# A gate's projection between the two halves of each pair's q and k, and every block of logits tied to a share of the pair's projections

## The chip, the core and the metric

The kernel runs on one core of a Trainium2 chip. The metric is the device time of one execution in microseconds (us). Five engines with queues of their own appear below: PE (matrix multiplies, with its weight loads shown apart as PEld), DVE (VectorE), ACT (ScalarE), POOL (GpSimd) and SP (which issues most DMAs). Each engine works through its own list in order.

## The reference, cut to what matters

One block with two mixers, for 1024 tokens of width 1024, in float32:

```python
h = _rmsnorm(x, norm_g)
u = h @ w_in                                   # all projections at once
u_a, u_b, u_g = split(u)                       # RWKV, forgetting attention, gates
y_a = _rwkv7_mixer(u_a, ...) @ w_out_a         # 8 heads of 64: a recurrence over the tokens
y_b = _fox_mixer(u_b, ...) @ w_out_b           # 8 heads of 64: causal softmax attention
merged = sigmoid(g_a) * y_a + sigmoid(g_b) * y_b
return _rmsnorm(x + merged @ w_out, final_norm_g)

# _fox_mixer: q and k are normalised per head, then for each block of queries
logits = q @ k.T * scale + cum[q] - cum[k]     # cum: running sum of log forget gates
p = softmax(where(causal, logits, -inf)); o = p @ v
```

## The kernel before, in words

All matrix products run as three products of split operands (high times high, high times low, low times high), so a projection of 128 columns for 512 tokens is 24 matmuls into one PSUM bank (`project`, L326 to L333). The transposed, normalised input lies on chip as `hTH` and `hTL`. The kernel has two kinds of work on PE. **Bulk**: projections that need nothing but `hT` and weights, namely r, k, v of the RWKV heads, 24 gate tiles (`gate_tile`, tiles `ps_gg`), v of the attention (`project_v`, `pfv`), and q and k of each pair of attention heads (`project_qk`, `pf`). **Latency-bound** work: small steps that wait for DVE, ACT or DMA after each matmul.

The RWKV part runs in four units (two groups of heads times two halves of the tokens). `prep` builds a unit's operands; its core is a triangular inverse made by a long series of DVE steps (`etmp`, `lt`, L663 and L667), a round trip through DRAM, then 32 small matmuls `pw` (L687), a copy by ACT, 32 more `pz` (L698), and a copy by ACT into `Tb`. `chain` then walks eight chunks; each step is `px` (L724), DVE, `pu` (L739), DVE, `po` (L749), DVE, and the next step needs the state that this one leaves. `norm_out` normalises a unit's output and ends in transposes `pt` (L796).

The attention goes by four pairs of heads. `project_qk` computes q and k of a pair for all tokens in eight blocks of 128 tokens; `norm_qk` scales them per head and transposes them, half of the tokens at a time (`pqk`, `pqq`, L971): the scaling of the first half is on POOL, of the second half on DVE (L967). The transposed q must also reach the other partitions, by a DMA on chip (`QA`, L988 and L989), and its low part goes through DRAM (`qlo`, L986, then `QZ`, L1002). `attend` takes blocks of 256 queries: logits `sc` (L1024 with `QA`, L1025 with `QZ`, L1029 the mask), a minimum on DVE (L1031), the exponential on ACT (L1035), a scaling on DVE (L1039), transposes `pt` (L1048) and the product with v, `po` (L1068, L1069). `merge` and the output projection follow.

A scheduler sets each engine's order when the program is built, by priorities: latency-bound work goes in as soon as it is ready in the scheduler's reckoning, bulk fills what is left. Where its reckoning would place a step too early, `not_before` ties the step to a place in the list of bulk matmuls (`laid_`); such a tie fixes the order on PE and makes nothing wait by itself. Gate tiles left over after the RWKV units (`RFILL`) are spread over the four pairs by `FPRE` and `FFILL`.

The weights have three slots of high and low parts (`WB`) and one landing buffer (`RB`). The projections of the RWKV and early attention part rotate over three PSUM banks (`RTAGS`).

Of the kernel before, what the change touches and what calls it, by code (L numbers as in the profile page):

```python
# [18 lines left out]
P = 128  # L19
S = 1024  # L20
# [31 lines left out]
QKFIRST = True  # L52
LATER = 1000000
PLACE = {
    "pw0_0": 179, "pw0_1": 294, "pw1_0": 398, "pw1_1": 502,
}
PACE = 0.3
PHPOOL = True
# [12 lines left out]
PACE0 = 0.0  # L71
WA1 = 0
MGB = 3
NQEARLY = True
ATTFIRST = True
T1B = 3
RFILL = [5, 5, 3, 3]
FPRE = [1, 0, 0, 2]
FFILL = [1, 2, 2, 0]


def rsqrt_newton(nc, y, x, t):
# [12 lines left out]
def kernel(  # L95
# [212 lines left out]
    transposed(1, range(KD))  # L308
    xctx.close()

    laid_ = []

    def laid(ins):
        laid_.append(ins.ins)

    def not_before(first, name):

        if name not in PLACE:
            return
        for ins in first:  # L320
            tc.add_manual_dep(
                ins, laid_[PLACE[name]].name,
                mybir.DependencyInfo(mybir.DependencyClass.NoSync, mybir.DependencyReason.DATA),
                reason="not_before",
            )
# [173 lines left out]
    def prep(pp_, n):  # L499
# [191 lines left out]
        for e, _, q1, q2 in half:  # L691
            nc.scalar.copy(TW[q2].rearrange("p c s -> p (c s)"), pw[q2, :])
        pz = ps_misc(f"pz{u}")
        for h in range(2):
            for c in range(UC):
                g = UC * h + c
                for e, _, q1, q2 in half:
                    nc.tensor.matmul(pz[q1, g * HB : (g + 1) * HB], TW[q2, g, :], Tb[q2, c, h, q2], start=True, stop=True)  # L698
        for e, _, q1, q2 in half:
            nc.scalar.copy(Tg[q1, :, :, q2], pz[q1, :].rearrange("p (h c t) -> p h c t", h=2, t=HB))  # L700
        return dict(AR=AR, Q=Q, BKt=BKt, SV=SV, AK=AK, WC=WC, bV=bV, s2c=s2c, lnw=lnw, pw=mms, sc=late_sc, pt=[])

    states = [rp.tile([P, 2, 2, C], F32, tag=f"state{j}", name=f"state{j}") for j in range(2)]
    for t in states:
# [129 lines left out]
    def project_v(cb):  # L834


        VC = 264
        KH = KD // 2
        ncol = VC if cb == 0 else 256
        c0 = COL_FV + 256 * cb  # L840
        vs_ = []
        for p in (2 * cb, 2 * cb + 1):
            vparts[p] = fpa[0].tile([P, 8, 2, P], F32R, tag="V", name=f"V{p}", bufs=VB)
            vs_.append(vparts[p])
        parts = []
        for kh in range(2):
            rs_ = slice(kh * KH * P, (kh + 1) * KH * P)
            wH = wpool.tile([P, KH, VC], F32R, tag="wH", name=f"wvH{cb}_{kh}", bufs=WB)[:, :, :ncol]
            wL = wpool.tile([P, KH, VC], F32R, tag="wL", name=f"wvL{cb}_{kh}", bufs=WB)[:, :, :ncol]
            w = wpool.tile([P, KH, VC], F32, tag="w", name=f"wv{cb}_{kh}", bufs=RB)[:, :, :ncol]  # L850
            nc.sync.dma_start(
                w[:, :, 0:256], w_in2[rs_, c0 : c0 + 256].rearrange("(k p) c -> p k c", p=P)
            )
            if cb == 0:
                nc.sync.dma_start(
                    w[:, :, 256:VC], w_in2[rs_, COL_FF : COL_FF + 8].rearrange("(k p) c -> p k c", p=P)
                )
# [52 lines left out]
    def project_qk(p):  # L910
# [41 lines left out]
        return xn, rr  # L952

    def norm_qk(p, xn, rr):
# [6 lines left out]
        cb = [rp.tile([P, S], F32, tag=("AK", "bV")[h], name=f"cb{p}_{h}") for h in range(2)]  # L961
        for h in range(2):
            src = cumd[8 * (2 * p + h) : 8 * (2 * p + h) + 8].rearrange("(o b) t -> o (b t)", o=1)
            nc.sync.dma_start(cb[h], src.broadcast_to([P, S]))
# [25 lines left out]
        return KA, QA, qlo, cb  # L990

    sc_tags = SCTAGS

    def attend(p, KA, QA, qlo, cb):
        for i in range(4):
            nb = 2 * i + 2

# [8 lines left out]
            for h, q in ((0, A), (1, B)):  # L1006
# [3 lines left out]
                for e in range(2):  # L1010
# [6 lines left out]
                    for g in range(ng):  # L1017
# [6 lines left out]
                        nc.tensor.matmul(sc[:, :mw], QA[:, h, qs], KA[:, h, ms], start=True, stop=False)  # L1024
# [131 lines left out]
    for i, (p, n) in enumerate(units):  # L1156
# [3 lines left out]
        with bulky():  # L1160
# [4 lines left out]
            if i + 1 == len(units):  # L1165
                project_v(0)
                forget()
                qk = project_qk(0)
        not_before(d["pw"], f"pw{p}_{n}")
        not_before(d["sc"], f"sc{p}_{n}")  # L1170
        if i:
            not_before(before["pt"], "pt%d_%d" % units[i - 1])
        before = d
        with order(-LATER):
            yv = chain(p, n, d)
        with order(LATER // 2 if i + 1 < len(units) else -LATER):
            norm_out(p, n, d, yv)
    bulk_tags[:] = FTAGS
    qk = norm_qk(0, *qk)
    def bulk_fox(p, nxt):  # L1180
        with bulky():
            fill(FPRE[p], 0)
            if p < 3:
                nxt = project_qk(p + 1)
            if p < 3 and NQEARLY:
                nxt = norm_qk(p + 1, *nxt)
            fill(FFILL[p], 0)
            if p < 3 and not NQEARLY:
                nxt = norm_qk(p + 1, *nxt)
        if p == 1 and ATTFIRST:  # L1190
            with order(LATER):
                project_v(1)
        return nxt

    for p in range(4):
        if not ATTFIRST:
            nxt = bulk_fox(p, None)
        with order(-LATER):
            attend(p, *qk)
        if ATTFIRST:  # L1200
            nxt = bulk_fox(p, None)
        qk = nxt
        if p == 0 and not ATTFIRST:
            with order(LATER):
                project_v(1)
# [68 lines left out]
```

## Time and profile before

| | |
|---|---|
| median of 3 runs | 1139.93 us (1131.49 to 1140.08) |
| profiled execution | 1135.76 us |
| its span, first to last instruction | 1133.9 us |
| PE busy | 1052.9 us, 93% of the span |
| DVE, ACT, POOL busy | 709.2, 459.9, 317.0 us |
| mean granted clock of PE | 0.968 of full speed |

The rows further down come from that one execution; times in them count from the start of its span. PE has two clock levels, 2.4 GHz (1.00) and 1.2 GHz (0.50); PEclk is the mean of what was granted in a stretch.

### The profile page before, as it was taken

To read this page: it belongs to the slowest core of one execution; us is meant where nothing else is said; L and a number is where in the kernel's file an instruction comes from. 1 tells how busy PE (TensorE), PEld (TensorE's weight loads), DVE (VectorE), ACT (ScalarE), POOL (GpSimd) and SP (SyncE) were. 2 spreads that over 40 slices of the span, in tenths; PEclk is the share of its full clock that TensorE was granted. 3 is DMA by queue.
4 is the path that set the end of the run, shared out by engine and by line. 5 is a ranking of instruction groups with operands and counts; after the bars stand their busy time and mean duration, and the time that the engine had idled before them with its cause. 6 is when DMAs were issued, how large, how long until landed. Compare 5 with 4: busy or idle time off the path is not lost. (4 is left out here: it accounts for less than half of the span.)

```text
span 1133.9 us, 18405 instructions
## 1 busy us (share of the span) xinstructions
PE 1052.9 (93%) x6591; PEld 871.7 (77%) x6591; DVE 709.2 (63%) x1855; ACT 459.9 (41%) x969; POOL 317.0 (28%) x467
## 2 busy tenths in 40 slices
PE   4989999999899999997998989979997999999997
PEld 3867777777677777777887877968896887887885
DVE  7414776699648883796678858652736823475145
ACT  6534323534243314431546636443544623223122
POOL 4420522252213421231113223222132222244400
PEclk9999999999989899998999989989998999999999
DMA  6256444144422433222024213232223126645133
GB/s 214 59 172 216 123 103 121 40 119 134 113 74 76 127 103 99 62 82 66 20 77 125 85 49 83 85 88 80 92 59 89 55 77 188 217 134 178 64 102 121
DMA packets 126684, 118.21 MB, mean 104 GB/s; under 512 B 33489, under 2 KB 91970, under 8 KB 126594
## 3 DMA queue, kind: packets, MB, share of 16 engines
q1 hardware_dynamic: 114304, 94.99, 29.1%
q10 hardware_dynamic: 11714, 21.52, 5.1%
q8 instruction: 52, 0.85, 0.3%
q0 software_dynamic: 576, 0.54, 0.2%
q14 instruction: 38, 0.31, 0.1%
HBM read 79.23 MB, written 35.68 MB: 101 GB/s over the span
## 5 line engine op out<-in xcount | busy, mean ns | idle before, releaser
L331 PE MATMUL ps_gg<-hTH,wH_gg 128*128 128x512 f32 x384 | 160.0, 417 | 0.8 <-DVE ql L982 0.6
L332 PE MATMUL ps_gg<-hTL,wH_gg 128*128 128x512 f32 x384 | 160.2, 417 | 0.0
L333 PE MATMUL ps_gg<-hTH,wL_gg 128*128 128x512 f32 x384 | 159.1, 414 | 0.0
L210 POOL TENSOR_TENSOR wL_gg<-w_gg,wH_gg 128x256 fp32r<-128x256 f32 x96 | 71.3, 774 | 194.2 <-ACT wH_gg L207 192.6
L331 PEld LDWEIGHTS ps_gg<-hTH,wH_gg 128*128 128x128 f32 x384 | 74.8, 195 | 15.5 <-issue 2.0
L333 PEld LDWEIGHTS ps_gg<-hTH,wL_gg 128*128 128x128 f32 x384 | 74.5, 194 | 13.9
L332 PEld LDWEIGHTS ps_gg<-hTL,wH_gg 128*128 128x128 f32 x384 | 74.6, 194 | 13.5
L938 PE MATMUL pf<-wqkL,hTH 128*128 128x256 f32 x256 | 73.7, 288 | 0.0
L939 PE MATMUL pf<-wqkH,hTL 128*128 128x256 f32 x256 | 73.7, 288 | 0.0
L937 PE MATMUL pf<-wqkH,hTH 128*128 128x256 f32 x256 | 73.5, 287 | 0.0
L396 ACT ACTIVATE gt<-ps_gg 128x512 f32<-128x512 f32 x40 | 23.9, 597 | 86.3 <-PE ps_gg L333 75.9
L1035 ACT ACTIVATE pr<-pr,mm 128x128 f32<-128x128 f32 (+3 forms) x64 | 49.9, 779 | 21.7 <-DVE mm L1031 19.4
L736 ACT ACTIVATE xw<-state,WC 64x64 f32<-64x64 f32 x112 | 38.7, 346 | 44.5 <-DVE state L756 37.3
L667 DVE TENSOR_TENSOR lt<-lt,etmp 64x30 f32<-64x30 f32 (+14 forms) x120 | 52.2, 435 | 3.7
L1228 PE MATMUL pz<-wo,mH 128*128 128x512 f32 (+1 forms) x136 | 52.4, 385 | 0.8 <-POOL wo L1097 0.8
L663 DVE TENSOR_TENSOR etmp<-lt 64x30 f32<-64x30 f32 (+14 forms) x120 | 47.7, 397 | 7.5 <-issue 4.0
L1227 PE MATMUL pz<-wo,mH 128*128 128x512 f32 (+1 forms) x136 | 51.8, 381 | 0.0
L1229 PE MATMUL pz<-wo,mL 128*128 128x512 f32 (+1 forms) x136 | 51.6, 379 | 0.0
L937 PEld LDWEIGHTS pf<-wqkH,hTH 128*128 128x128 f32 x256 | 49.2, 192 | 0.0
L938 PEld LDWEIGHTS pf<-wqkL,hTH 128*128 128x128 f32 x256 | 49.1, 192 | 0.0
L939 PEld LDWEIGHTS pf<-wqkH,hTL 128*128 128x128 f32 x256 | 49.0, 191 | 0.1
L1024 PE MATMUL sc<-KA,QA 128*128 128x384 f32 (+4 forms) x96 | 36.7, 390 | 12.0 <-DMA QA<-QA 11.9
(332 smaller groups left out, 2832.5 us busy)
## 6 DMA issues: line engine op xcount, KB each, us to landing
w_gg<-in_w_in_dram SPq DMA_DIRECT2D x24, 512.0 KB, 3.8
gab<-gt ACTq DMA_DIRECT2D x48, 256.0 KB, 2.0
ring<-gab SPq DMA_DIRECT2D x32, 256.0 KB, 3.1
xt<-in_x_dram SPq DMA_DIRECT2D x8, 512.0 KB, 6.1
wqk<-in_w_in_dram SPq DMA_DIRECT2D x16, 256.0 KB, 2.9
cb<-cumd SPq DMA_DIRECT2D x8, 512.0 KB, 4.1
ring<-yab SPq DMA_DIRECT2D x16, 256.0 KB, 3.7
ring<-in_w_out_dram SPq DMA_DIRECT2D x16, 256.0 KB, 3.1
```

The source lines that it names most:

```text
L210: nc.gpsimd.tensor_sub(wL[:, k], w[:, k], wH[:, k])
L331: nc.tensor.matmul(ps, wH[:, k, :], rH[:, k, ts_], start=(k == 0), stop=False)
L332: nc.tensor.matmul(ps, wH[:, k, :], rL[:, k, ts_], start=False, stop=False)
L333: laid(nc.tensor.matmul(ps, wL[:, k, :], rH[:, k, ts_], start=False, stop=(k == nk - 1)))
L667: nc.vector.tensor_add(lt3[:, :s, s + 1 :], lt3[:, :s, s + 1 :], tm)
L937: nc.tensor.matmul(ps, hTH[:, k, bs], wH[:, kk, :], start=(k == 0), stop=False)
L938: nc.tensor.matmul(ps, hTH[:, k, bs], wL[:, kk, :], start=False, stop=False)
L939: laid(nc.tensor.matmul(ps, hTL[:, k, bs], wH[:, kk, :], start=False, stop=(k == KD - 1)))
L1035: nc.scalar.activation(pr[:, :w], pr[:, :w], AF.Exp, bias=last, scale=-1.0, accum_out=mm[:, 2:3])
L1227: nc.tensor.matmul(ps, mH[:, k, bs], oH[:, k, c], start=(k == 0), stop=False)
L1228: nc.tensor.matmul(ps, mH[:, k, bs], oL[:, k, c], start=False, stop=False)
L1229: nc.tensor.matmul(ps, mL[:, k, bs], oH[:, k, c], start=False, stop=(k == KD - 1))
```

## The change

It does four things. The inverse's second group of matmuls `pz` gets a tie of its own, so that 12 to 30 bulk matmuls stand between `pw` and `pz`; two groups of logits of `prep` (`sc1_0`, `sc1_1`) are tied as well. The gate tiles move: one more for each of the last two RWKV units (`RFILL`), and one between the two halves of every pair's q and k (`next_qk`); only pair 3 keeps two in front. The last unit's `norm_out` moves between the halves of pair 0, with its transposes six places behind. And each of the eight logits blocks of a pair (four query blocks, two heads) is tied to a place in the pair's bulk: the first at 16 places after the first half's transposes begin, the others at shares of the rest that grow with the block's size (`SCAT`, `SPREAD`). A place is three matmuls of 512 columns, or six of 256. The loads of `cb` move from `norm_qk` to `attend`; on SP they keep their places.

```diff
 PLACE = {
-    "pw0_0": 179, "pw0_1": 294, "pw1_0": 398, "pw1_1": 502,
+    "pw0_0": 179, "pz0_0": 183, "pw0_1": 296, "pz0_1": 301, "sc1_0": 352, "pw1_0": 404, "pz1_0": 409,
+    "sc1_1": 457, "pw1_1": 525, "pz1_1": 535,
 }
...
-NQEARLY = True
-ATTFIRST = True
+QKAT = ((-2, 0), (-4, 0))
+PTAT = 6
+SCAT = 16
+SPREAD = 0.9
 T1B = 3
-RFILL = [5, 5, 3, 3]
-FPRE = [1, 0, 0, 2]
-FFILL = [1, 2, 2, 0]
+RFILL = [5, 5, 4, 4]
+FPRE = [0, 0, 0, 2]
+FFILL = [0, 0, 0, 0]
...
+    def beside(first, steps):
+
+        pins.append((first, len(laid_) - 1, int(steps * HALF)))
+
+    def place_all():
+        for first, j, cols in pins:
+            while cols > 0 and j + 1 < len(laid_):
+                j += 1
+                cols -= cols_[j]
+            while cols < 0:
+                cols += cols_[j]
+                j -= 1
+            for ins in first:
+                tc.add_manual_dep(
+                    ins, laid_[j].name,
+                    mybir.DependencyInfo(mybir.DependencyClass.NoSync, mybir.DependencyReason.DATA),
+                    reason="not_before",
+                )
...
-        for n in range(2):
+
+        def half(n, places):
             xg = xn[n].rearrange("p b (g i) -> p (b g) i", i=HD)
...
-                for j in range(4):
-                    nc.tensor.transpose(pq[:, j * P : (j + 1) * P], xn[n][:, j, c * P : (c + 1) * P], ident)
+                first = [
+                    nc.tensor.transpose(pq[:, j * P : (j + 1) * P], xn[n][:, j, c * P : (c + 1) * P], ident).ins
+                    for j in range(4)
+                ]
+                beside(first[:1], places[1 - c])
...
+        not_before(d["pz"], f"pz{p}_{n}")
         not_before(d["sc"], f"sc{p}_{n}")
...
+    starts = []
+
+    def next_qk(p, xr, between=lambda: None):
+
+        KA, QA, qlo, half = norm_qk(p, *xr)
+        starts.append(len(laid_) - 1)
+        half(0, QKAT[0])
+        between()
+        with order(LATER) if p == 0 else nullcontext():
+            gate_tile(gates.pop(0))
+        half(1, QKAT[1])
+        return KA, QA, qlo
+
+    def last_norm():
+        with order(-LATER):
             norm_out(p, n, d, yv)
-    bulk_tags[:] = FTAGS
-    qk = norm_qk(0, *qk)
...
+        beside(d["pt"], PTAT)
+
+    qk = next_qk(0, xr, last_norm)
+    for p in range(4):
+        with order(-LATER):
+            attend(p, *qk)
         with bulky():
             fill(FPRE[p], 0)
             if p < 3:
-                nxt = project_qk(p + 1)
-            if p < 3 and NQEARLY:
-                nxt = norm_qk(p + 1, *nxt)
+                qk = next_qk(p + 1, project_qk(p + 1))
             fill(FFILL[p], 0)
...
+        end = starts[p + 1] if p < 3 else len(laid_) - 1
+        room = sum(cols_[starts[p] + 1 : end + 1]) - SCAT * HALF
+        for k, first in enumerate(blocks[p]):
+            i, h = divmod(k, 2)
+            if k == 0 or SPREAD:
+                pins.append(([first], starts[p], int(SCAT * HALF + SPREAD * room * (i + h) * (i + 1) / 20)))
```

How the order on PE moves is shown at three places. First, the start of pair 1: the transposes of the first half of its k and q (`pqk1_0`, `pqq1_0`), its first logits `sc1_0` and the second half's transposes. Before:

```order
L971 MATMUL pqk1_0_6638<-ident_89,xn1_0_6370 128x128 x4
L971 MATMUL pqq1_0_6647<-ident_89,xn1_0_6370 128x128 x4
L1024 MATMUL sc1_0_0_0_0_6758<-KA1_6630,QA1_6631 128x256
L1024 MATMUL sc1_0_0_1_0_6767<-KA1_6630,QA1_6631 128x256
L331 MATMUL ps_gg9_0_6692<-hTH_72,wH_gg9_6683 128x512
L332 MATMUL ps_gg9_0_6692<-hTL_73,wH_gg9_6683 128x512
L333 MATMUL ps_gg9_0_6692<-hTH_72,wL_gg9_6684 128x512
L331 MATMUL ps_gg9_0_6692<-hTH_72,wH_gg9_6683 128x512
L971 MATMUL pqk1_1_6661<-ident_89,xn1_1_6500 128x128 x4
L971 MATMUL pqq1_1_6670<-ident_89,xn1_1_6500 128x128 x4
```

The same place in the change, in two pieces; between them stand 46 more matmuls of gate tile 11, 48 in all:

```order
L990 MATMUL pqk1_0_6764<-ident_89,xn1_0_6500 128x128 x4
L990 MATMUL pqq1_0_6773<-ident_89,xn1_0_6500 128x128 x4
L348 MATMUL ps_gg11_0_6795<-hTH_72,wH_gg11_6786 128x512
L349 MATMUL ps_gg11_0_6795<-hTL_73,wH_gg11_6786 128x512
L350 MATMUL ps_gg11_0_6795<-hTH_72,wL_gg11_6787 128x512
```

```order
L350 MATMUL ps_gg11_1_6823<-hTH_72,wL_gg11_6787 128x512
L1053 MATMUL sc1_0_0_0_0_6888<-KA1_6760,QA1_6761 128x256
L1056 MATMUL sc1_0_0_0_0_6888<-KA1_6760,QZ1_0_6878 128x256
L1060 LDWEIGHTS identb_440
L1060 MATMUL sc1_0_0_0_0_6888<-cmask_442,identb_440 128x128
L1053 MATMUL sc1_0_0_1_0_6897<-KA1_6760,QA1_6761 128x256
L1056 MATMUL sc1_0_0_1_0_6897<-KA1_6760,QZ1_0_6878 128x256
L1060 LDWEIGHTS identb_440
L1060 MATMUL sc1_0_0_1_0_6897<-cmask_442,identb_440 128x128
L990 MATMUL pqk1_1_6852<-ident_89,xn1_1_6630 128x128 x4
L990 MATMUL pqq1_1_6861<-ident_89,xn1_1_6630 128x128 x4
```

A whole gate tile now lies between the first half's transposes and the first logits, which take `QA` and `QZ` one after the other; the second half's transposes come behind them. Pairs 2 and 3 look alike with tiles 12 and 13.

Second, where the attention's v begins (`pfv0_0`), behind gate tile 7 before:

```order
L331 MATMUL ps_gg7_1_4866<-hTH_72,wH_gg7_4829 128x512
L332 MATMUL ps_gg7_1_4866<-hTL_73,wH_gg7_4829 128x512
L333 MATMUL ps_gg7_1_4866<-hTH_72,wL_gg7_4830 128x512
L867 MATMUL pfv0_0_4916<-wvH0_0_4896,hTH_72 128x264
L868 MATMUL pfv0_0_4916<-wvL0_0_4897,hTH_72 128x264
```

and behind gate tile 9 in the change, so that 96 more matmuls of 512 columns (tiles 8 and 9) precede it:

```order
L348 MATMUL ps_gg9_1_4996<-hTH_72,wH_gg9_4959 128x512
L349 MATMUL ps_gg9_1_4996<-hTL_73,wH_gg9_4959 128x512
L350 MATMUL ps_gg9_1_4996<-hTH_72,wL_gg9_4960 128x512
L889 MATMUL pfv0_0_5046<-wvH0_0_5026,hTH_72 128x264
L890 MATMUL pfv0_0_5046<-wvL0_0_5027,hTH_72 128x264
```

Third, the middle of the last unit's chain (`px1_1`, `pu1_1`, `po1_1`), where the projection of v ends and that of pair 0's q and k (`pf0`) begins. Before, from the last matmul of v:

```order
L869 MATMUL pfv0_7_5126<-wvH0_1_4906,hTL_73 128x264
L739 MATMUL pu1_1_3_5546<-xw1_1_5465,Tb_430 128x64 x2
L749 MATMUL po1_1_3_5551<-SV1_1_4312,BKt1_1_4311 128x128 x2
L765 MATMUL py1_1_3_5558<-SV1_1_4312,Q1_1_4309 64x64 x16
L724 MATMUL px1_1_4_5576<-state0_432,AR1_1_4308 128x128 x2
L739 MATMUL pu1_1_4_5587<-xw1_1_5465,Tb_430 128x64 x2
L749 MATMUL po1_1_4_5592<-SV1_1_4312,BKt1_1_4311 128x128 x2
L896 MATMUL pcs_5165<-lf_438,tri_5162 128x64
L897 MATMUL pcs_5165<-lf_438,tri_5162 128x64
L937 MATMUL pf0_0_0_5206<-wqkH0_0_5184,hTH_72 128x256
```

and in the change:

```order
L891 MATMUL pfv0_7_5256<-wvH0_1_5036,hTL_73 128x264
L771 MATMUL po1_1_3_5681<-SV1_1_4377,BKt1_1_4376 128x128 x2
L787 MATMUL py1_1_3_5688<-SV1_1_4377,Q1_1_4374 64x64 x16
L746 MATMUL px1_1_4_5706<-state0_432,AR1_1_4373 128x128 x2
L761 MATMUL pu1_1_4_5717<-xw1_1_5595,Tb_430 128x64 x2
L771 MATMUL po1_1_4_5722<-SV1_1_4377,BKt1_1_4376 128x128 x2
L746 MATMUL px1_1_5_5729<-state1_433,AR1_1_4373 128x128 x2
L918 MATMUL pcs_5295<-lf_438,tri_5292 128x64
L919 MATMUL pcs_5295<-lf_438,tri_5292 128x64
L761 MATMUL pu1_1_5_5740<-xw1_1_5595,Tb_430 128x64 x2
L771 MATMUL po1_1_5_5745<-SV1_1_4377,BKt1_1_4376 128x128 x2
L746 MATMUL px1_1_6_5752<-state0_432,AR1_1_4373 128x128 x2
```

There `pu1_1_6` follows, and only then `pf0`: the steps from `po1_1_3` to `pu1_1_6` have no bulk between them, where before it was those from `pu1_1_3` to `po1_1_4`.

## Rows read from the trace of the kernel before

**Rows 1.** The page, part 1: busy time of PE, share of span, instructions.

```profile
PE 1052.9 (93%) x6591; PEld 871.7 (77%) x6591; DVE 709.2 (63%) x1855; ACT 459.9 (41%) x969; POOL 317.0 (28%) x467
```

**Rows 2.** Waits of PE, whole span: total us, how many, longest.

```profile
PE sc L1024 <- DMA QA<-QA: 11.9, 3, 4.0
PE pqk L971 <- DVE xn L967: 10.1, 4, 3.5
PE pfv L867 <- DVE lf L878: 7.1, 1, 7.1
...
PE pw L687 <- DVE TW L679: 3.5, 4, 1.4
PE pz L698 <- ACT TW L692: 2.9, 2, 2.4
...
PE pt L796 <- DVE yv L791: 2.0, 1, 2.0
...
PE psc L587 <- DVE BK L578: 1.4, 1, 1.4
...
PE ps_gg L331 <- DVE ql L982: 0.6, 1, 0.6
```

**Rows 3.** Windows at half clock: us, busy PE, PEld, DVE, ACT, POOL, PEclk, DMA.

```profile
525.80:532.70 6.90, 4.87 (x22) 4.90 (x23) 3.48 (x18) 0.00 (x0) 0.00 (x0) 0.51 0.30 56
590.70:594.20 3.50, 3.50 (x19) 3.42 (x19) 0.43 (x1) 2.96 (x7) 1.63 (x3) 0.51 0.53 195
604.30:607.80 3.50, 3.08 (x15) 2.62 (x16) 2.49 (x14) 2.34 (x8) 0.84 (x4) 0.51 0.31 92
672.60:679.50 6.90, 5.29 (x17) 3.91 (x17) 4.23 (x9) 1.63 (x3) 2.11 (x4) 0.51 0.40 114
747.70:758.00 10.30, 6.29 (x19) 5.24 (x20) 7.36 (x13) 3.59 (x5) 3.39 (x5) 0.50 0.40 103
860.30:870.70 10.40, 6.59 (x20) 5.46 (x21) 7.17 (x13) 3.59 (x5) 3.52 (x6) 0.51 0.39 104
307.40:317.70 10.30, 7.92 (x82) 5.84 (x77) 1.38 (x2) 4.44 (x7) 2.78 (x4) 0.50 0.45 145
372.20:382.50 10.30, 10.30 (x41) 8.62 (x41) 7.02 (x15) 2.76 (x5) 4.62 (x6) 0.50 0.43 127
```

**Rows 4.** Windows at full clock: pair 0's attention, and a stretch of pure 512-column matmuls.

```profile
608.00:668.00 60.00, 59.06 (x432) 53.19 (x431) 43.11 (x126) 34.61 (x84) 16.31 (x34) 1.00 0.25 75
...
975.00:1000.00 25.00, 25.00 (x109) 20.10 (x108) 12.03 (x18) 5.13 (x7) 7.37 (x9) 1.00 0.59 194
```

**Rows 5.** Timeline of PE at pair 1's start: start, us, operation, idle before.

```profile
667.87 0.60 PE L971 MATMUL pqq<-ident,xn 128*128 128x128 f32 x4
672.43 0.59 PE L1024 MATMUL sc<-KA,QA 128*128 128x256 f32 x2 [3.96 <-DMA QA<-QA]
```

**Rows 6.** Timeline of SP at pair 1.

```profile
678.65 2.39 SPq L1002 DMA_DIRECT2D QZ<-qlo  x4
```

**Rows 7.** DMA issues: out, in, count, KB each, median us to landing.

```profile
QZ<-qlo SPq DMA_DIRECT2D x32, 64.0 KB, 2.4
```

**Rows 8.** Timeline of DVE: the last step of the last unit's inverse.

```profile
526.88 0.20 DVE L667 TENSOR_TENSOR lt<-lt,etmp 64x30 f32<-64x30 f32 x1
```

**Rows 9.** Timeline of PE in the last unit's chain, behind v's last matmul.

```profile
555.28 0.81 PE L749 MATMUL po<-SV,BKt 128*128 128x128 f32 x4 [0.37 <-DVE SV L741]
...
557.11 0.80 PE L724 MATMUL px<-state,AR 128*128 128x128 f32 x4
558.99 0.63 PE L739 MATMUL pu<-xw,Tb 128*128 128x64 f32 x4 [1.08 <-DVE xw L729]
559.99 1.23 PE L749 MATMUL po<-SV,BKt 128*128 128x128 f32 x4 [0.38 <-DVE SV L741]
```

**Rows 10.** Groups by line: shapes, count, busy us, mean ns, idle before.

```profile
L1035 ACT ACTIVATE pr<-pr,mm 128x128 f32<-128x128 f32 (+3 forms) x64 | 49.9, 779 | 21.7 <-DVE mm L1031 19.4 <-PE sc L1025 1.2 <-DVE mm L1038 0.4
...
L1039 DVE TENSOR_SCALAR pr<-pr,mm 128x128 f32<-128x128 f32 (+3 forms) x64 | 35.1, 553 | 0.8
```

More of the change, by code (lines that the diff above doesn't have):

```diff
@@ L309, with laid @@
     xctx.close()
-    laid_ = []
-    def laid(ins):
+    laid_, cols_, pins = [], [], []
+    def laid(ins, cols=HALF):
         laid_.append(ins.ins)
+        cols_.append(cols)
     def not_before(first, name):
[L318 to L325, printed above, removed]
+        if name in PLACE:
+            pins.append((first, PLACE[name], 0))
+    def beside(first, steps):
[14 more added lines that the diff above has]
+                )
     def project(ps, wH, wL, rH, rL, n, nk=KD):
@@ L693, in prep @@
         pz = ps_misc(f"pz{u}")
+        pzs = []
         for h in range(2):
@@ L697, in prep @@
                 for e, _, q1, q2 in half:
-                    nc.tensor.matmul(pz[q1, g * HB : (g + 1) * HB], TW[q2, g, :], Tb[q2, c, h, q2], start=True, stop=True)
+                    pzs.append(
+                        nc.tensor.matmul(
+                            pz[q1, g * HB : (g + 1) * HB], TW[q2, g, :], Tb[q2, c, h, q2], start=True, stop=True
+                        ).ins
+                    )
         for e, _, q1, q2 in half:
             nc.scalar.copy(Tg[q1, :, :, q2], pz[q1, :].rearrange("p (h c t) -> p h c t", h=2, t=HB))
-        return dict(AR=AR, Q=Q, BKt=BKt, SV=SV, AK=AK, WC=WC, bV=bV, s2c=s2c, lnw=lnw, pw=mms, sc=late_sc, pt=[])
+        return dict(pz=pzs, AR=AR, Q=Q, BKt=BKt, SV=SV, AK=AK, WC=WC, bV=bV, s2c=s2c, lnw=lnw, pw=mms, sc=late_sc, pt=[])
     states = [rp.tile([P, 2, 2, C], F32, tag=f"state{j}", name=f"state{j}") for j in range(2)]
@@ L868, in project_v @@
                 nc.tensor.matmul(o, hTH[:, k, bs], wL[:, kk, :], start=False, stop=False)
-                laid(nc.tensor.matmul(o, hTL[:, k, bs], wH[:, kk, :], start=False, stop=(k == KD - 1)))
+                laid(nc.tensor.matmul(o, hTL[:, k, bs], wH[:, kk, :], start=False, stop=(k == KD - 1)), QB)
             pvv = pv[:, 0:256].rearrange("p (g h i) -> p g h i", g=2, h=2)
@@ L938, in project_qk @@
                     nc.tensor.matmul(ps, hTH[:, k, bs], wL[:, kk, :], start=False, stop=False)
-                    laid(nc.tensor.matmul(ps, hTL[:, k, bs], wH[:, kk, :], start=False, stop=(k == KD - 1)))
+                    laid(nc.tensor.matmul(ps, hTL[:, k, bs], wH[:, kk, :], start=False, stop=(k == KD - 1)), QB)
                 nc.scalar.copy(xt[:, b], ps)
@@ L960, in norm_qk @@
         qlo = dp.tile([P, S], F32, tag="qlo", name=f"qlo{p}", bufs=2)
[L961 to L964, printed above, removed]
-        for n in range(2):
+        def half(n, places):
             xg = xn[n].rearrange("p b (g i) -> p (b g) i", i=HD)
@@ L989, in norm_qk, with attend @@
             nc.sync.dma_start(QAf[A, 1], QAf[B, 1])
-        return KA, QA, qlo, cb
+        return KA, QA, qlo, half
     sc_tags = SCTAGS
-    def attend(p, KA, QA, qlo, cb):
+    blocks = [[] for _ in range(4)]
+    def attend(p, KA, QA, qlo):
+        cb = [rp.tile([P, S], F32, tag=("AK", "bV")[h], name=f"cb{p}_{h}") for h in range(2)]
+        for h in range(2):
+            src = cumd[8 * (2 * p + h) : 8 * (2 * p + h) + 8].rearrange("(o b) t -> o (b t)", o=1)
+            nc.sync.dma_start(cb[h], src.broadcast_to([P, S]))
         for i in range(4):
@@ L1023, in attend @@
                         end = g + 1 == ng
-                        nc.tensor.matmul(sc[:, :mw], QA[:, h, qs], KA[:, h, ms], start=True, stop=False)
+                        qk = nc.tensor.matmul(sc[:, :mw], QA[:, h, qs], KA[:, h, ms], start=True, stop=False)
+                        if e == 0 and g == 0:
+                            blocks[p].append(qk.ins)
                         nc.tensor.matmul(
@@ L1167 @@
                 forget()
-                qk = project_qk(0)
+                xr = project_qk(0)
         not_before(d["pw"], f"pw{p}_{n}")
+        not_before(d["pz"], f"pz{p}_{n}")
         not_before(d["sc"], f"sc{p}_{n}")
@@ L1175 @@
             yv = chain(p, n, d)
-        with order(LATER // 2 if i + 1 < len(units) else -LATER):
-            norm_out(p, n, d, yv)
-    bulk_tags[:] = FTAGS
-    qk = norm_qk(0, *qk)
-    def bulk_fox(p, nxt):
+        if i + 1 < len(units):
+            with order(LATER // 2):
+                norm_out(p, n, d, yv)
+    bulk_tags[:] = FTAGS
+    starts = []
[10 more added lines that the diff above has]
+        with order(-LATER):
+            norm_out(p, n, d, yv)
+        beside(d["pt"], PTAT)
[3 more added lines that the diff above has]
+            attend(p, *qk)
         with bulky():
@@ L1183, in bulk_fox @@
             if p < 3:
-                nxt = project_qk(p + 1)
-            if p < 3 and NQEARLY:
-                nxt = norm_qk(p + 1, *nxt)
+                qk = next_qk(p + 1, project_qk(p + 1))
             fill(FFILL[p], 0)
-            if p < 3 and not NQEARLY:
-                nxt = norm_qk(p + 1, *nxt)
-        if p == 1 and ATTFIRST:
+        if p == 1:
             with order(LATER):
                 project_v(1)
-        return nxt
     for p in range(4):
[L1196 to L1205, printed above, removed]
+        end = starts[p + 1] if p < 3 else len(laid_) - 1
[4 more added lines that the diff above has]
+                pins.append(([first], starts[p], int(SCAT * HALF + SPREAD * room * (i + h) * (i + 1) / 20)))
     bulk_tags[:] = TTAGS
     tc.cur_priority += LATER
+    place_all()
     mH, mL, wos = merge()
```

## The prediction

> **What bounds the kernel now.** I read the page's busy times first. PE is busy for 1052.9 us of the 1133.9 us span [rows 1], and the change adds no matmul, so only two things can be won: time in which PE waits, and time in which it works at half clock. The list of PE's waits comes next [rows 2]: see there that most of them have one place, the start of the attention's pairs. The first logits wait for the copy of q between partitions (`QA`, 11.9 us in three waits of up to 4.0), the second half's transposes for DVE's scaling (`xn`, 10.1 us in four), v's projection once for 7.1 us, the last `norm_out` 2.0, and 0.6 behind `ql`. That makes 31.7 us. The windows of half clock are third [rows 3]: the first six follow these waits, and PE was busy for 4.87 + 3.50 + 3.08 + 5.29 + 6.29 + 6.59 = 29.6 us in them. At 1.2 instead of 2.4 GHz, half of that, 14.8 us, was lost. Last, what lies between: pair 0's attention ran 60 us at full clock with PE busy for 59.06 [rows 4]. The interleaving of logits and projections inside a pair has nothing to give; its start has.
>
> The sum is made against the profiled execution, 1135.8 us (span 1133.9). The median of the runs shown is 1139.9, 0.4% higher; they scatter by 0.8%, so I forecast the same number for the median. About 1% is what a measurement of this kernel can tell from no change.
>
> **The change, part by part.**
>
> *Start of a pair.* In pairs 1 to 3 the first logits now stand 48 matmuls of 512 columns behind the transposes. A stretch of such matmuls shows 109 in 25.00 us [rows 4], 0.229 us each, so the cover is 11.0 us. `QA` needs 4.0 us [rows 5], and DVE's scaling, which ended the second half's wait, is also done by then: PE's longest wait for it was 3.5 us [rows 2]. All three `QA` waits, the four `xn` waits (pair 0 gets a tile in its gap too) and the 0.6 go: 22.6 us. What is late next is `QZ`. Its matmul now stands directly behind the `QA` one, where before 13 gate matmuls and the second half's transposes lay between. In pair 1 `pqq` ends at 667.87 + 0.60 = 668.5, the `QZ` loads are issued from 678.65 [rows 6] and land 2.4 us later [rows 7], at 681.05: 12.6 us after the transposes, against 11.0 of cover. I charge 1.5 us for each of three pairs, 4.5. The bounds are 0 (the gate tile's rows and SP's queue shift a little) and 4.0 each, the longest `QA` wait, 12. The `cb` loads keep their places on SP, so they cost nothing; if they were pulled ahead of `QA`, SP would hold it up by an issue.
>
> *Projection of v.* Its PSUM banks were freed by DVE, whose list has the whole inverse of the last unit first; that ended at 527.08 [rows 8], and PE stood 7.1 us [rows 2]. Now 96 gate matmuls (22.0 us), which ACT empties, come first. The unit's own start moves too: in the order its chain predecessor ends 25 matmuls later, 5.7 us. So v's fourth block arrives 22.0 - 5.7 - 7.1 = 9.2 us behind the freeing instead of 7.1 ahead of it. The wait goes. `norm_out`'s 2.0 goes with its transposes six places into a gate tile.
>
> *Half clock at these places.* With the waits gone I take all 14.8 us back. By the Trainium skill, TensorE: Matmul & The Clock Gate, Terms, the penalty is the whole throttled time by one half; the six windows last 41.5 us, which would make it 20.8 and the time 1089. The trace disagrees as far as part of that time was waiting and is counted already.
>
> *The last unit's chain.* This is what the change pays. Five more hops have no bulk between them (`px5`, `pu5`, `po5`, `px6`, `pu6`). From [rows 9] a hop takes 1.83 us from `po` to `px`, 1.88 to `pu`, 1.00 to `po`. The bare stretch was `pu3` to `po4`, 1.00 + 1.83 + 1.88 + 1.00 = 5.7 us; it becomes `po3` to `pu6`, twice 4.71 plus 3.71, 13.1. The difference is 7.4. Of this the five hops' own matmuls, 0.80 + 0.63 + 0.81 + 0.80 + 0.63 = 3.7 us, were paid before too, so 3.7 is the low end. On the high end PE comes out of 13 half-empty microseconds at half clock; the widest window after a pair's wait lost 3.3 us of work, and all 7.4 with it makes 10.7. I take 6, nearer the low end because the hops' matmuls were paid in either order.
>
> *`pw` and `pz`.* With 12 or more matmuls between them `pz` no longer waits for ACT (2.9 us). But in unit 1 `pw` is reached 6 matmuls (1.4 us) later, while the chain that its DVE work waits for ends 11 matmuls (2.5 us) later, so `pw`'s 3.5 us grow by 1.1. Net gain 1.8, between 0 and 2.9. The half clock at 307 stays.
>
> *`sc1_0` tied.* The 1.4 us wait of `psc` goes; the half clock behind it (10.30 us of work, 5.2 lost) [rows 3] may stay or go, and with one small wait as its only cause I take half: 4.0 in all, between 0 and 6.6.
>
> *The end.* The last logits now end about 5 matmuls before the projections, where 38 places covered them. Their store stands ahead of the merge's loads on SP. I charge 1 us, with 0 and 4.0 (the longest DMA wait) as bounds.
>
> Sum: 22.6 + 7.1 + 2.0 + 14.8 + 1.8 + 4.0 = 52.3 won, 4.5 + 6 + 1 = 11.5 paid. 1135.8 - 40.8 = **1095 us**.
>
> **The rivals.**
>
> *The wait moves to `QZ`, and the chain costs its upper end.* For it: 12.6 us against 11.0 of cover. Against: one pair's rows, 1.6 us late, are all that speaks for the first part, and an order of hops without any use of the bulk behind it for the second. With 12 for 4.5 and 10.7 for 6 it gives 1107, and with half clock after each of three waits (at most 3.3 each) 1117.
>
> *The clock keeps what it takes.* More, shorter groups of small matmuls between projections could hold PE at 1.2 GHz for as long as now, whatever the waits: 14.8 us stay, 1110. Against: pair 0's 60 us were as mixed as the new order and ran at 1.00 [rows 4]. The Trainium skill, TensorE: Matmul & The Clock Gate, A second HAM failure mode, says that small idles between groups that cycle through PSUM banks make the clock swing. By that rule it is this case; that stretch speaks against it.
>
> *More is won.* If both further windows of half clock go (4.0 and the other 2.6 us), `QZ` waits for nothing and the chain costs 3.7, it is 1082.
>
> *Slower than before.* Each softmax must be done before its transposes. If the ties put the logits so late that PE stands for ACT's exponential and DVE's scaling, 0.78 + 0.55 = 1.33 us [rows 10], in each of 64 halves, that is 85 us and 1180. It outweighs the gain from 0.64 us each. Against: in pair 0's attention the same steps left PE idle for 0.94 us in 60 [rows 4], with fewer projections between them than the new order has.
>
> *It does not do what it says.* The ties set an order in the scheduler's reckoning, and if engines run otherwise, new waits of the same size come elsewhere: about 1136.
>
> **How the numbers follow.** Forecast (1086 to 1107) 0.60; `QZ` and chain dear 0.12; the clock 0.10; more won 0.08; slower 0.05; no change 0.05. The range leaves out the last two and the outer ends of the others: 1081 to 1117. All cases but the last two lie below 1128.5, 1% under the median: faster 0.90, same 0.05, slower 0.05.
>
> **What would show it.** In the new profile PE's waits should have no `sc` behind `QA`, no `pqk` behind `xn`, no `pfv` behind `lf`; small waits of `sc` behind `QZ` at three pair starts; `pw` about 1 us more in unit 1, `pz` none. PE's chain from `po3` to `pu6` of the last unit should stand bare for about 13 us, with half clock at its end and none at the pair starts. I am wrong if PE waits for `pr` or `PHL` in the attention, if half clock persists there without waits, or if the bare chain costs over 11 us.

## The result, and the profile after

| | median | runs |
|---|---|---|
| before | 1138.99 us | 4, 1131.5 to 1140.1 |
| changed | 1122.63 us | 4, 1121.4 to 1128.1 |

The ratio is 0.988, with a 95% interval of 0.984 to 0.992: faster by 1.2%, which is 16 us where the sum had 41, and outside the range (1081 to 1117). The profiled execution took 1122.8 us (span 1121.1), 13.0 less than the one of before.

PE's busy time on the page of the changed kernel is that of [rows 1], 1052.8 for 1052.9 us; no work was saved. What changed is in PE's waits (total us, how many, longest), the answer to [rows 2]:

```profile
PE sc L1056 <- DMA QZ<-qlo: 12.0, 5, 3.7
...
PE ps_gg L348 <- DVE last_gg L381: 4.4, 2, 3.0
PE psc L604 <- DVE Q L610: 3.8, 3, 2.6
...
PE ps_gg L348 <- DVE gt L375: 3.0, 3, 1.3
PE pw L704 <- DVE TW L696: 2.6, 2, 1.7
...
PE ps_gg L348 <- DVE gt L417: 1.4, 1, 1.4
```

The waits of `sc` for `QA`, `pqk` for `xn`, `pfv` for `lf`, and `pz` for `TW` have no row any more, as forecast. But `QZ` takes 12.0 us where 4.5 were charged, `psc` did not lose its wait, and the gate tiles (`ps_gg`) wait 8.8 us for DVE between 260 and 320 us, a place that had none. `psc` now waits for `Q` where it waited for `BK`, 3.8 us against 2.0 in all.

The windows at half clock (us, busy time of PE, PEld, DVE, ACT, POOL, then PEclk), the answer to [rows 3]:

```profile
381.70:388.50 6.80, 6.24 (x24) 5.67 (x25) 5.41 (x11) 0.59 (x1) 5.21 (x8) 0.50 0.32 85
432.90:439.70 6.80, 6.80 (x73) 5.25 (x74) 0.33 (x1) 1.56 (x3) 0.00 (x0) 0.50 0.55 161
576.30:589.90 13.60, 10.87 (x45) 9.86 (x45) 7.50 (x30) 5.66 (x16) 2.78 (x4) 0.50 0.30 79
630.90:637.70 6.80, 6.49 (x27) 5.32 (x28) 4.14 (x18) 3.93 (x10) 0.76 (x3) 0.50 0.40 107
774.20:781.00 6.80, 6.30 (x29) 6.11 (x30) 1.97 (x8) 2.63 (x6) 3.12 (x6) 0.50 0.36 107
873.20:876.60 3.40, 3.05 (x14) 2.87 (x15) 1.59 (x8) 1.65 (x6) 1.35 (x2) 0.50 0.64 195
```

A further window, 3.4 us from 504.5 on, lost 1.7 us. In the attention (the last three rows) half of 6.49 + 6.30 + 3.05, that is 7.9 us, is still lost; the last three attention windows of [rows 3] lost 9.1. So 1.2 us of clock came back there, and each of the three windows begins at the end of a `QZ` wait, of 3.0, 3.7 and 2.6 us.

Three stages in windows, with the same columns: the units from 255 us on, the last unit up to pair 0's start, and the attention. First the kernel before:

```profile
255.00:470.00 215.00, 206.23 (x1425) 164.03 (x1424) 151.69 (x372) 78.57 (x167) 52.90 (x69) 0.95 0.35 100
470.00:610.00 140.00, 124.35 (x1007) 109.70 (x1007) 108.23 (x294) 56.22 (x133) 39.08 (x55) 0.94 0.25 69
610.00:980.00 370.00, 346.17 (x2174) 298.37 (x2173) 216.12 (x615) 176.50 (x404) 95.16 (x181) 0.96 0.31 94
```

then the changed kernel:

```profile
255.00:470.00 215.00, 200.34 (x1369) 158.49 (x1368) 143.88 (x357) 76.58 (x159) 61.48 (x73) 0.97 0.36 103
470.00:610.00 140.00, 134.35 (x1060) 117.87 (x1059) 98.08 (x276) 50.75 (x122) 36.45 (x49) 0.94 0.25 69
610.00:980.00 370.00, 353.62 (x2228) 303.81 (x2227) 238.20 (x659) 187.22 (x426) 99.99 (x195) 0.98 0.33 101
```

Window less PE's busy time is its idle time: 8.8 became 14.7 in the units, 15.7 became 5.7 around `pfv`, 23.8 became 16.4 in the attention. The gain lies where `pfv` waited; the attention gave 7.4 us, a third of what it had, and the units lost 5.9.

SP's queue at pair 1 (start, duration, operation), which answers [rows 6]:

```profile
691.74 0.48 SPq L1011 DMA_DIRECT2D QA<-QA  x1
695.74 0.39 SPq L941 DMA_DIRECT2D wqk<-in_w_in_dram  x1
696.22 0.46 SPq L1008 DMA_DIRECT2D qlo<-ql  x1
696.72 0.48 SPq L941 DMA_DIRECT2D wqk<-in_w_in_dram  x1
700.11 2.39 SPq L1031 DMA_DIRECT2D QZ<-qlo  x4
```

and PE there (idle before in brackets), for [rows 5]:

```profile
688.79 0.60 PE L990 MATMUL pqq<-ident,xn 128*128 128x128 f32 x4
...
702.44 0.38 PE L1056 MATMUL sc<-KA,QZ 128*128 128x256 f32 x1 [1.59 <-DMA QZ<-qlo]
```

From the transposes' end, 689.39, to the `QZ` matmul are 13.05 us; the forecast had 12.6. Between lie two transfers one behind the other (`ql` to `qlo`, `qlo` to `QZ`), and the first is queued on SP behind a load of weights. In pair 2 it is the second:

```profile
766.83 0.33 SPq L1008 DMA_DIRECT2D qlo<-ql  x1
770.77 0.94 SPq L941 DMA_DIRECT2D wqk<-in_w_in_dram  x2
771.82 2.38 SPq L1031 DMA_DIRECT2D QZ<-qlo  x4
```

### The profile page after: what moved, and what is told of

It is laid out like the page before. It is cut to its first block, busy times and chain, and to the rows that moved or that the text cites. A ratio compares the mean times of both kernels' runs of the same rounds, so it can differ in the third digit from the quotient of the medians.

```text
span 1121.1 us, 18391 instructions
## 1 busy us (share of the span) xinstructions
PE 1052.8 (94%) x6591; PEld 871.9 (78%) x6591; DVE 706.1 (63%) x1855; ACT 460.8 (41%) x969; POOL 317.7 (28%) x467
## 5 line engine op out<-in xcount | busy, mean ns | idle before, releaser
L350 PE MATMUL ps_gg<-hTH,wL_gg 128*128 128x512 f32 x384 | 156.1, 407 | 0.0
L349 PE MATMUL ps_gg<-hTL,wH_gg 128*128 128x512 f32 x384 | 155.6, 405 | 0.0
L213 POOL TENSOR_TENSOR wL_gg<-w_gg,wH_gg 128x256 fp32r<-128x256 f32 x96 | 75.2, 814 | 195.5 <-ACT wH_gg L210 149.9
L350 PEld LDWEIGHTS ps_gg<-hTH,wL_gg 128*128 128x128 f32 x384 | 73.0, 190 | 14.8
L1062 DVE CUSTOM_DVE_ANT_0 pr<-sc,cb 128x128 f32<-128x128 f32 (+3 forms) x64 | 34.2, 535 | 38.5 <-PE sc L1060 26.9
L1079 PE MATMUL pt<-ident,pr 128*128 128x128 f32 x288 | 48.8, 277 | 2.3 <-DVE pr L1070 1.1
L684 DVE TENSOR_TENSOR lt<-lt,etmp 64x30 f32<-64x30 f32 (+14 forms) x120 | 48.2, 402 | 3.7
```

Source lines behind the costliest of these rows:

```text
L213: nc.gpsimd.tensor_sub(wL[:, k], w[:, k], wH[:, k])
L349: nc.tensor.matmul(ps, wH[:, k, :], rL[:, k, ts_], start=False, stop=False)
L350: laid(nc.tensor.matmul(ps, wL[:, k, :], rH[:, k, ts_], start=False, stop=(k == nk - 1)))
L1079: nc.tensor.transpose(pt[:, o : o + P], probs[e][:, kb * P : (kb + 1) * P], ident)
```

## The experiments

The theory: `QZ` comes later than its cover (the bulk between the transposes and the first logits, 16 steps), and the half clock in the attention comes with its waits. The rival: the new mixture of logits and projections holds the clock down or makes the softmax late, and the `QZ` waits only stand in its place. Edits are against the changed kernel; ratios are against the kernel before, measured anew beside each group of runs, with 95% intervals (the change: 0.988, 0.984 to 0.992). Differences of medians in us carry the scatter of both.

**More cover.** e1, then e6:

```diff
-SCAT = 16
+SCAT = 28      # e6: 22
```

> The first logits of a pair stand 28 steps (84 projections of 512 columns, about 19 us) behind the transposes instead of 16 (11 us). Theory (the copies QZ are later than the cover): the 12.0 us that PE waits for QZ fall under 2, and the half clock at 631, 774 and 873 us (17 us long, 8 us of work lost) goes with them: 1103 to 1111 us. Rival (the logits and their softmax get too little room and the wait only moves): QZ falls as well, but pt behind pr or po behind PHL takes its place: 1118 to 1126 us.

Measured: 1111.7 us, 0.977 (0.973 to 0.980), 0.7 above the theory's end. No `QZ` row is left, and the half clock at 631, 774 and 873 us is gone. In its place came waits of `pf` for ACT's squares, 4.4 us, and two windows of half clock behind them, at 642 and 709 us, that lost 3.1.

> 22 steps, between the change's 16 and the 28 tried. Theory (6 steps, 4.1 us, cover the longest QZ wait of 3.7): QZ waits under 2 us, and the pf waits for ACT's squares that 28 steps showed (4.4 us) are smaller, as the logits have more room: 1107 to 1112 us. Rival (each step more buys, also beyond the QZ wait): near the middle of 1122.6 and 1111.7, 1115 to 1119.

Measured: 1120.3 us, 0.985 (0.981 to 0.989), outside both. PE waits for `QZ` no more, but over 10 us of other waits came in the attention, most of them in these two rows:

```profile
PE sc L1053 <- DVE mm L1062: 6.7, 2, 5.2
PE pt L1079 <- DVE pr L1070: 4.5, 3, 4.2
```

The mechanism is in ACT's list: at 638.0 the cast of a gate's weights (`wH_gg`) had waited 5.6 us for its load, which SP had issued only at 632.0, behind the last `yab` and two `QZ`. The squares stand behind the cast, DVE's sums behind the squares, the softmax behind those. SP's queue is late for more than `QZ`.

**One transfer instead of two** (e5): the cover stays 16 steps.

```diff
+                if key == "q" and n == 0:
+                    QZ = rp.tile([P, 2, QB], F32R, tag="yg", name=f"QZ{p}_0")
+                    QZf = QZ.bitcast(F32)
+                    for h, q, qo in halves:
+                        nc.gpsimd.memset(QZf[qo, h, :], 0.0)
+                        nc.sync.dma_start(QZf[q, h, :], ql.bitcast(F32)[q, 0:QB])
+                    first_qz.append(QZ)
                 if key == "q":
                     nc.sync.dma_start(qlo[:, HS[n]], ql.bitcast(F32))
...
+            if i == 0:
+                QZ = first_qz.pop(0)
+            else:
...
```

> The ties stay (first logits 16 steps behind the transposes), but the first QZ of a pair is copied straight from ql, one transfer instead of two behind one another (ql to qlo to QZ), and ahead of qlo on SP. Theory (QZ is late by its second transfer and by what SP has ahead of it): the three first waits of pairs 1 to 3 (1.6 + 3.7 + 2.6 = 7.8 us) go, and the half clock behind two of them (about 4 us of work): 1109 to 1114 us; pair 0's 3.0 and pair 3's later 1.2 stay. Rival (the cover of 11 us is too short for any way over SP): sc still waits 4 us or more for QZ or QA, 1117 to 1124.

Measured: 1114.6 us, 0.981 (0.976 to 0.986), 0.6 above the theory's end; by itself it is not separated from the change, as the intervals overlap. PE waits 1.9 us in all for `QZ`, and from 593 us to the end of the attention the clock is whole. `pt` waits more for `pr`, 5.7 us for 1.1. Both together (e12: this edit and `SCAT = 28`):

> The direct copy with 28 steps, the ties of the units as in the change. Theory (QZ's lateness is all that 28 steps buy): within 3 us of either alone, 1110 to 1115 us. Rival (they add, the later logits also free PE from the first softmax): 1104 to 1109.

Measured: 1105.2 us, 0.971 (0.968 to 0.975). The rival's side: they add. The attention of e12 in one window:

```profile
593.00:1060.00 467.00, 458.80 (x2811) 392.38 (x2810) 293.54 (x769) 217.43 (x489) 140.11 (x224) 1.00 0.35 106
```

458.8 of 467 us busy at a granted clock of 1.00, with the same mixture of short groups of logits between projections. So the mixture does not hold the clock down; the half clock in the attention went with the `QZ` waits, in e5 and e12 both. Not every wait brings it: in e5 PE stood 3.19 us for `pr` at 775.50, and the clock stayed at 1.00.

**The shares of the later blocks** (e4: `SPREAD = 0.0`).

> Only the first logits of each pair are tied, the shares of the other blocks are dropped. Theory (the shares bring nothing by themselves, as pair 0 ran full without them): 1119 to 1126 us, QZ waits as now. Rival 1 (the shares cost, by more changes between logits and projections): projections of q and k take 3 us less, 1115 to 1119. Rival 2 (the shares bring the gain): logits run ahead, softmax falls behind, PE waits for pr, and a pair's end is bare of logits: 1130 or more.

Measured: 1122.4 us, 0.985 (0.981 to 0.989): the theory. Within this noise, which of the later logits stand beside which projection is worth nothing.

**The ties in the units.** e2 drops one, e11 all that are new or moved in the first three units, e13 the two of `psc`:

```diff
 e2:  -"pz0_0": 183,
 e11: -"pz0_0": 183, "pw0_1": 296, "pz0_1": 301, "sc1_0": 352, "pw1_0": 404, "pz1_0": 409, "sc1_1": 457,
      +"pw0_1": 294, "pw1_0": 398,
 e13: -"sc1_0": 352, "sc1_1": 457,
```

> Only the tie of pz0_0 is dropped, which puts unit 0's chain and VectorE's series for unit 1 back where they were. Theory (VectorE is the bound between 260 and 330 us, whatever PE waits in): the gate tiles' 8.8 us of waits for VectorE fall under 3, but pw of unit 1 waits about 3 us again and the half clock near 307 us is back: within 3 us of 1122.6. Rival (the later series is a cost by itself): the 8.8 us go and nothing comes back but a pz wait of 0.7: 1113 to 1117 us.

Measured: 1120.6 us, 0.984 (0.982 to 0.987): the theory's time. The gates' 8.8 us are 1.5, but `pz` waits 3.0 in the same stretch, and `psc` of unit 2 3.5 where it waited 2.6. So the tie mostly exchanges waits, only not for those of the `pw` that the theory named. Half clock stands at 319, but that is no mark of this edit (last section).

> All ties of the first three units that the change added or moved are dropped again; what is left is the attention's part, v's projection behind gate tiles and the last unit's pw and pz. Theory (these ties only change in which instruction PE waits for VectorE): 1119 to 1126 us. Rival 1 (they win what the prediction gave them, 5.8 us): 1127 to 1131. Rival 2 (they cost): 1113 to 1118.

Measured: 1117.2 us, 0.981 (0.978 to 0.985): in the range of the second rival, that the ties cost, though its interval still touches that of the change. Which of them, e13 was to tell:

> Of the change's early ties only the two of psc are dropped; pz0_0, pz0_1, pz1_0 and the moved pw stay. Theory (what the early ties cost, about 5 us, comes with unit 0's and unit 2's chains ending later, not with psc): 1119 to 1125 us. Rival (psc's tie holds back VectorE's series, which starts from it, and is the cost): 1114 to 1118.

Measured: 1111.5 us, 0.978 (0.975 to 0.982), below even the rival's range: `psc`'s ties are the cost. Which of the two costs more was not tried. How, DVE's timeline shows. The changed kernel, unit 2:

```profile
369.00 1.21 DVE L808 TENSOR_REDUCE stat<-yq 128x16 f32<-128x1024 f32 x1
...
378.71 1.07 DVE L593 TENSOR_SCALAR ta<-ta,col 128x512 f32<-128x512 f32 x1
379.70 1.74 DVE L811 TENSOR_TENSOR yv<-yv,stat 128x1024 f32<-128x1024 f32 x1
381.37 0.41 DVE L610 TENSOR_TENSOR QL<-psc,mask 128x256 f32<-128x256 f32 x1
...
386.53 0.41 DVE L610 TENSOR_TENSOR Q<-psc,mask 128x256 f32<-128x256 f32 x1
```

and PE there:

```profile
382.26 3.75 PE L604 MATMUL psc<-AR,BK 64*128 64x128 f32 x16 [2.65 <-DVE Q L610]
```

In e13, the same operations of DVE:

```profile
370.10 1.22 DVE L808 TENSOR_REDUCE stat<-yq 128x16 f32<-128x1024 f32 x1
...
376.19 0.42 DVE L610 TENSOR_TENSOR QL<-psc,mask 128x256 f32<-128x256 f32 x1 [0.22 <-PE psc L604]
...
380.72 0.41 DVE L610 TENSOR_TENSOR Q<-psc,mask 128x256 f32<-128x256 f32 x1
```

With the tie, DVE's list has `norm_out`'s long operations ahead of the emptying of `psc`, so PE stands 2.65 us for a bank, and `psc` is empty at 386.94 instead of 381.13, although the stretch began 1.10 earlier: 6.9 us. DVE's whole inverse follows from there. So `pw` of unit 2 waits 2.6 us, and half clock stands behind the two waits, at 382 and 433. In e13 no `pw` row is left and the clock is whole from 318 to 567 us.

The clock's part in this is not shown. e16 (below) drops the same two ties and has the same wait of `psc` for `BK` here as e13, 1.18 us, but its profile stood at half clock from 376 to 388 us:

```profile
315.00:400.00 85.00, 83.82 (x640) 67.26 (x635) 58.85 (x142) 36.26 (x77) 27.05 (x36) 0.92 0.31 90
```

The kernel before stood so at 372 [rows 3]. In e16 `psc` is empty 4.0 us sooner than with the ties, counted from the same operation (L808), where e13 has 6.9.

**The last unit's chain.** e3 and e7 fill it with bulk from both sides, e8 gives unit 2 a tile:

```diff
 e3: -RFILL = [5, 5, 4, 4]; FPRE = [0, 0, 0, 2]      +RFILL = [5, 5, 4, 3]; FPRE = [0, 0, 0, 3]
 e7: +RFILL = [5, 5, 4, 5]; FPRE = [0, 0, 0, 1]      and bulk_tags turned by 2 ahead of project_v(0)
 e8: +RFILL = [5, 5, 5, 4]; FPRE = [0, 0, 0, 1]      sc1_0 +5, pw1_0 and pz1_0 +8, sc1_1, pw1_1 and pz1_1 +10
```

> One gate tile of the last unit goes to the last pair, so that the banks of v's and q/k's projections fall on the chain's hops in another turn: in PE's order two bare stretches of two hops each stand where six in a row stood. Theory (the bare chain costs its idle time and the half clock behind it): idle time between 573 and 590 us falls from 4.7 to under 3, the half clock of 13.7 us there shrinks to at most 7: 1115 to 1119 us. Rival (the chain is bound by VectorE's and ScalarE's hops, the bulk only fills it and is missing later): within 2 us of 1122.6.

Measured: 1121.8 us, 0.985 (0.982 to 0.989): no gain, the rival's value. Most of the chain is covered (1.1 us idle from 573 to 590 us), and `pfv` waits again:

```profile
PE pfv L889 <- DVE lf L900: 6.6, 1, 6.6
```

> A gate tile of the last pair goes to the last unit (5 there instead of 4), and the banks turn by two, so that in PE's order two hops of the last chain are bare instead of six, and v's projection stays behind gate tiles. Theory (chain and pfv's wait are one shortage of other work beside the last unit's VectorE series; one tile more fills it): idle time from 530 to 620 us falls from 4.6 to under 2.5 and the half clock there (5.4 us lost) to under 2: 1114 to 1119 us. Rival (the last pair, a tile poorer, gives it back in waits of pt or po): 1120 to 1125.

Measured: 1120.4 us, 0.984 (0.980 to 0.988): unclear, at the rival's lower end, and only in part for its reason (`po` waits 2.7 us for ACT). No wait in the chain is over 0.4 us, but PE's idle time from 530 to 620 us rose from 4.6 to 6.0, as `pct` at 598 us stands for the same DVE:

```profile
PE pct L927 <- DVE stat L809: 4.5, 1, 4.5
```

> The same tile goes to unit 2 instead, with the ties behind it moved by the time that psc and pw wait there (5 to 10 steps). Theory (VectorE bounds unit 2: PE waits 2.7 us for Q, 2.6 us for TW and loses 6.5 us to half clock, which more work beside it fills): these waits under 2 us, 1113 to 1118 us. Rival (the tile only moves the waits to the next unit): 1120 to 1125.

Measured: 1117.4 us, 0.982 (0.977 to 0.988): in the theory's range, not separated from the change. `pw` and `psc` wait 1.6 us in all, but `norm_out`'s transposes wait 4.1 for DVE's `yv`.

**Together.** e9: e5 and e8. e10: the same with 28 steps. e14: e12 with e11's table. e15: that with e8's tile, `pw` at 297, 410 and 535. e16: e12 and e13. e17: e16 with e8's tile, `pw1_1` at 535, `pz1_1` at 545. e18: e17 without `pz0_0`.

> The direct copy of the first QZ and the tile moved to unit 2 with its ties, together. Theory (the two gains, 8 and 5 us, lie in different stages): they add, 1108 to 1112 us, QZ waits under 2.5 us, psc and pw under 2. Rival (the later stages take the first gain back): 1113 to 1118.

Measured: 1106.9 us, 0.972 (0.969 to 0.976): they add, and come out 1.1 below the theory's range.

> The same with 28 steps of cover instead of 16. Theory (the first logits' softmax is no longer waited for: pt behind pr, 5.7 us with the direct copy alone, falls under 2): 1104 to 1110 us. Rival (28 steps press the rest of the logits together, as the 4.4 us of pf behind ACT's squares showed): no faster than with 16 steps, 1109 to 1114.

Measured: 1100.9 us, 0.966 (0.961 to 0.970), 3.1 below the theory's range: `pt` waits 0.8 us for `pr` instead of 4.5.

> The direct copy of QZ, 28 steps, and the early ties of the units dropped. Theory (dropping the ties gave 5 us in a stage of its own): 1098 to 1103 us, 5 below the same with the ties. Rival (that gain was the clock's scatter): 1104 to 1108.

Measured: 1100.5 us, 0.967 (0.964 to 0.970): the theory.

> The last one with the tile from the last pair in unit 2 as well, pw of the units moved by 3, 12 and 10 steps. Theory (the tile fills what VectorE's series leaves bare in units 2 and 3, as with the ties): 1093 to 1099 us. Rival (tile and dropped ties heal the same wait): 1099 to 1104.

Measured: 1097.3 us, 0.964 (0.961 to 0.967): the theory's range; its interval overlaps that of e14.

> The direct copy, 28 steps, and psc's two ties dropped; nothing else differs from the change. Theory (late QZ and psc's ties are separate costs, 17 and 11 us): they add, 1094 to 1099 us, which is the forecast's place. Rival (the clock takes part of it back): 1100 to 1106.

Measured: 1097.5 us, 0.965 (0.963 to 0.968). It is the theory's range, and inside the forecast's (1086 to 1107): the two failed steps undone put the change where the forecast had it. The two gains, 17.5 and 11.1 us, come to 25.1 together, 3.5 less than their sum; dropping the ties is worth 7.7 of it here (from e12).

> The same with the last pair's tile in unit 2 and the last unit's ties 10 steps later, so that two hops of its chain are bare instead of six. Theory (the bare chain costs 4 us or more): 1089 to 1095 us. Rival (unit 2 needs no tile once psc is free): equal to the one without the tile within 2 us.

Measured: 1093.8 us, 0.963 (0.960 to 0.965), the fastest. That the chain costs the 3.7 us between e16 and e17 is not settled, as the intervals overlap. Its stages:

```profile
255.00:315.00 60.00, 52.69 (x332) 40.84 (x331) 44.97 (x102) 17.22 (x31) 18.34 (x20) 0.97 0.46 128
...
530.00:610.00 80.00, 76.92 (x713) 72.09 (x712) 42.39 (x141) 32.32 (x88) 11.35 (x16) 0.96 0.20 56
610.00:980.00 370.00, 362.71 (x2281) 311.37 (x2280) 254.15 (x687) 191.06 (x432) 110.93 (x198) 1.00 0.36 110
```

Idle time is left mainly before 315 us, 7.3, where the gates wait for DVE; the attention has 7.3 in 370.

> The last one without pz0_0's tie. Theory (between 260 and 330 us VectorE bounds PE in either order): within 3 us of the one with the tie. Rival (the gate tiles' 6.7 us of waits are a net cost): 4 to 7 us faster.

Measured: 1099.2 us, 0.966 (0.963 to 0.968). Slower by 5 us at the medians, intervals overlapping: neither theory, and no sign that dropping this tie would win the gates' waits.

## Why the prediction was wrong

- **Starts of the pairs, 22.6 won:** right. `QA`, `xn` and `ql` have no row.
- **`QZ`, 4.5 paid:** the step that failed first; 12.0 came. For pair 1 the working held (1.5 charged, 1.6 measured), but that pair's price was put on all. In pair 2 the load of `wqk` waited for POOL until 770.77, ahead of `QZ` at 771.82: 3.7. In pair 3 it was 2.6, and 1.2 at a later block. Pair 0, charged nothing, paid 3.0, as SP stood 4.7 us at `yab` for POOL's `yo`. That the upper bound, 12, was met is chance: the three pairs it was worked out for paid 7.8.
- **Half clock, 14.8 won:** rested on no wait being left. The first three windows (5.7) went, and 1.2 came back in the attention; 7.9 us stayed behind the `QZ` waits. e5 and e12 give them back by earlier copies and more cover. Late `QZ` with its clock is worth 17.5 us (e12). The rule by which small idles between groups that cycle through PSUM banks make the clock swing (the Trainium skill, TensorE: Matmul & The Clock Gate, A second HAM failure mode) did not show here: e12's 467 us ran at 1.00.
- **`sc1_0` tied, 4.0 won:** failed in sign. With `sc1_1`, whose tie had no term in the sum, it cost 11.1 us (e13), or 7.7 once `QZ` is on time (e12 to e16). I looked at what PE waits for and not at what DVE does first once `psc` comes later.
- **`pw` and `pz`, 1.8 won:** `pz`'s wait went, as said. The forecast of 1 us more in unit 1's `pw` was wrong, and so was its reading of the 3.5 us, which were the waits of units 1 and 2 together, 1.7 and 1.8. Unit 1's are gone, unit 2's are 2.6, and the gates wait 8.8 us before that. e2 shows that most of it is an exchange. The half clock at 307 (4.0 lost), which the sum kept, is not in this profile, but other executions of the same code have it (last section).
- **`pfv` and `norm_out`, 9.1 won:** right; e3 brings 6.6 back by taking the tile away.
- **The last chain, 6 paid:** right in size. Six hops were bare, as told, 573 to 586 us, with 4.3 us idle and 5.4 lost to half clock, 9.7 in all. The bare steps of the kernel before had 2.4 idle from 553 to 566 us, and about 1.6 lost to a window of half clock at 560 that [rows 3] does not list, so the difference is 5.7. Of it 1.9 is idle time, where 3.7 was the low end, and 3.8 is clock; that the total agrees so well is partly chance. It was not to be had back by filling this place alone: DVE, late by then, was waited for elsewhere (e3, e7).
- **The end, 1 paid:** nothing; the merge waits 0.9 us for `ya`, as before (1.0).

The rival of dear `QZ` and chain (1107 to 1117) had this mechanism, with the half clock in it. It missed the `psc` ties, without which the change runs at 1111.5, inside its range.

## What to carry over

When a wait is covered by a count of other work, work out the next wait's path for each place apart: how many transfers lie behind one another, and what stands ahead of them in the issuing queue there. A tie on PE is also a change of another engine's list; ask what that engine does first while the tied work is away. Where a wait is left, let the range hold the half clock that can come with it, and credit the clock only where none is.

## What was not expected of the hardware

The same code is not granted the same clock each time. The edits of e4, e5, e6, e7, e12 and e13 concern only what comes after 345 us. From 255 to 345 us the profile of the change shows a granted clock of 1.00, theirs show 0.94 each, though PE idles as long (9.1 us in the change, 9.0 in e12). In the longer window shown for the change above, where its 0.97 is from the windows at 382 and 433 alone, e12 has

```profile
255.00:470.00 215.00, 200.51 (x1348) 158.29 (x1347) 140.66 (x345) 72.41 (x151) 61.32 (x73) 0.94 0.35 102
```

So a window of half clock that is there in one profile and gone in the next is no evidence for an edit by itself. The whole times scatter with it: e7's runs took 1113.7 us at a mean clock of 0.985 and 1121.1 at 0.978. The clock is not all of the scatter, as e14's took 1097.8 us at 0.978 and 1104.8 at 0.979. Half a per cent between two medians is not yet a difference.
